# Weight sums at set places in GpSimd's queue, an earlier load of the up block, and a shorter modulation in a two-layer hybrid transformer

## The chip, the cores and the metric

One core of one Trainium2 chip runs the whole kernel. The metric is the device time of one execution in microseconds (us). The engines are TensorE (PE, matrix products; PEld is its weight load), VectorE (DVE), ScalarE (ACT), GpSimd (POOL) and SyncE (SP), whose queue issues all transfers (DMAs) here. Each engine works through its own queue in order and waits on semaphores for the others.

## The reference, cut to what matters

512 latent tokens and 256 context tokens of width 1024 go through two layers. In a layer a conditioning vector gives six modulation vectors; three mixers (window attention, gated linear attention, neighbourhood attention) work on the modulated norm, then comes the feed-forward network (FFN), hidden width 2816. The context is updated in layer 0 only; layer 1 uses it just for keys, values and the context part of the gated linear attention.

```python
def swiglu(h, w_in, w_out):
    gate, up = jnp.split(h @ w_in, 2, axis=-1)
    return (jax.nn.silu(gate) * up) @ w_out
...
    for l in range(DEPTH):
        last = l == DEPTH - 1
        mod = (jax.nn.silu(c) @ w_ada[l] + b_ada[l])[:, None, :]
        mod_c = (jax.nn.silu(c_ctx) @ w_ada[l] + b_ada[l])[None, None, :]
        sh_m, sc_m, gt_m, sh_f, sc_f, gt_f = jnp.split(mod, 6, axis=-1)
        shc_m, scc_m, gtc_m, shc_f, scc_f, gtc_f = jnp.split(mod_c, 6, axis=-1)
        h = rmsnorm(x, norm_mix[l]) * (1.0 + sc_m) + sh_m
        hc = rmsnorm(xc, norm_mix[l]) * (1.0 + scc_m) + shc_m
...
        hf = rmsnorm(x, norm_ffn[l]) * (1.0 + sc_f) + sh_f
        x = x + gt_f * swiglu(hf, w_ffn_in[l], w_ffn_out[l])
        if not last:
            hfc = rmsnorm(xc, norm_ffn[l]) * (1.0 + scc_f) + shc_f
            xc = xc + gtc_f * swiglu(hfc, w_ffn_in[l], w_ffn_out[l])
```

## The kernel before

**Products.** Activations lie with channels on the partitions and tokens in the free direction. Each f32 operand is split into a high and a low part (`fp32r`), and a product is three passes: high weight by high activation, high by low, low by high. A weight block of 128x1024 is loaded by SP into one of three buffers `wr` (line 317), ACT casts its high half `wh` (L346), and DVE subtracts to get the low half `wl` (L350). `run_items` goes through a list of items: it loads as far as buffers allow, splits up to three items ahead, and calls the item's products. Results land in the PSUM tiles `g` and `h` in rotation. Activations are split by ACT (L183) and DVE (L184).

**Seven products.** In the FFN of layer 0 the hidden blocks 3 to 21 (nineteen of them) take seven products of 128x384 where eight would do it directly, in the manner of Strassen and Winograd, over the two halves of the 768 tokens and of the block pair G (gate) and U (up). `seven` writes a block as four items: `i1` (two products from G), `i2` (two, from the sums `ta`), `i3` (two, from half of U and half of `tb`) and `i4` (one, from `tb`). The sums of weights `ta` and `tb` are made by POOL, four operations on 128x512 for each block (L483). `sums()` writes those that have their operands and a free buffer into the program; before, it is called wherever a split is written. The gate block's buffer comes free after the last of the four, the up block's after `i3`'s split. SiLU times up is `evac` (L1830): one operation on POOL for each half of the tokens (x = 0 after `i3`, x = 1 after `i4`).

**Groups.** The blocks are worked in groups of 3, 3, 3, 3, 3, 3 and 4. Behind each comes an output product: eight items `w_fo`, each with 512 and 256 columns, added to the residual by DVE (L1794). The first item `i1` of the next group's first block (`begun`) stands ahead of the output product, the rest behind it.

**Late modulation.** `ada_late` makes the six modulation vectors of layer 1 beside the FFN of layer 0. It takes 96 steps: SP loads a 128x512 block of weights (`wad`, two buffers, L696), DVE multiplies it with the vectors of two streams, latents and context, and adds to `wac` (L706 the first, L708 the others: one operation for each stream). After eight steps sixteen or eight small products with `sel` gather the rows on PE, ACT copies them (`ada`, L721), products with `k_sel` turn them (`o`), and DVE writes `mod` (L757). A step is written into the program when the kernel's own program clock has moved on by the number that the generator yields; what is left at the start of layer 1 is written by `drain` in `close_phase`.

Of the kernel before, what the change touches and what calls it, by code (L numbers as in the profile page):

```python
# [22 lines left out]
KT = D // 128  # L23
# [120 lines left out]
class Net:  # L144
# [155 lines left out]
    def run_items(self):  # L300

        ws = [n for n, it in enumerate(self.items) if it.weights]
        raw, split, early = {}, {}, set()
        st = {"d": 0, "s": 0, "q": 0, "lo": None}

        def load():
            while st["d"] < len(ws):
                it = self.items[ws[st["d"]]]
                if it.w is None:
                    raw[st["d"]] = None  # L310
                    early.add(st["d"])
                    st["d"] += 1
                    continue
                if len({id(t) for q, t in raw.items() if q not in early} | {id(t) for t in self.held}) > 2:
                    break
                t = self.base.tile([128, 1024], F32, tag="wr", name=self.nm("wr"), bufs=3)
                self.nc.sync.dma_start(t[:, :it.nk * 128], it.w)
                raw[st["d"]] = t
                if it.got:
                    it.got(t)  # L320
                st["d"] += 1

        def split_lo():
            f, st["lo"] = st["lo"], None
            if f:
                f()
            self.sums()

        def split_hi(k):

            self.sums()
            while st["s"] < len(ws) and st["s"] <= k:
                q = st["s"]
                it = self.items[ws[q]]
                if it.raw:
                    st["s"] += 1
                    continue
                if st["lo"] or q not in raw or (len(split) > 1 and q != st["q"]):
                    return
                parts = it.parts() if it.parts else [(raw[q], 0, it.nk * 128)]  # L340
                if parts is None:
                    return
                hi = self.base.tile([128, 1024], F32R, tag="wh", name=self.nm("wh"), bufs=3)
                lo = self.base.tile([128, 1024], F32R, tag="wl", name=self.nm("wl"), bufs=3)
                for r, c, n in parts:
                    self.nc.scalar.copy(hi[:, c:c + n], r[:, :n])  # L346

                def lo_part(q=q, it=it, parts=parts, hi=hi, lo=lo):
                    for r, c, n in parts:
                        self.nc.vector.tensor_tensor(out=lo[:, c:c + n], in0=r[:, :n],  # L350
                                                     in1=hi[:, c:c + n].bitcast(F32), op=ALU.subtract)
                    del raw[q]
                    if it.done:
                        it.done()
                    split[q] = (hi, lo)
                st["lo"] = lo_part
                st["s"] += 1

        def ahead(lo=True):
            load()  # L360
            split_hi(st["q"] + 3)
            if lo:
                split_lo()
                load()

        def preload(q, pool=None):
            it = self.items[ws[q]]
            if pool is None:
                t = self.base.tile([128, 1024], F32, tag="wr", name=self.nm("wr"), bufs=3)
            else:  # L370
                t = pool.tile([128, 1024], F32, tag="W0", name=self.nm("W0"), bufs=16)
                early.add(q)
            self.nc.sync.dma_start(t[:, :it.nk * 128], it.w)
            raw[q] = t
            st["d"] = max(st["d"], q + 1)
        self.preload = preload
        self.ahead, self.split_lo = ahead, lambda: (split_lo(), load())
        for it in self.items:
            if not it.weights:
                it.fn()  # L380
                continue
            q = st["q"]
            load()
            if not it.raw:
                split_lo()
                if q not in split:
                    split_hi(q)
                    split_lo()
            load()
            if it.raw:  # L390
                it.fn(raw.pop(q))
            else:
                w = split.pop(q)
                it.fn(*w)
            st["q"] += 1

    def gemm(self, w, nk, subs):

        def sub(wh, wl, mov, n, evac):
            ps = self.gemm_psum()  # L400
            for kt in range(nk):
                xh, xl = mov(kt)
                if any(lo.tensor is xl.tensor for lo, _ in self.late):
                    self.flush()
                s = slice(kt * 128, kt * 128 + 128)
                last = kt == nk - 1
                self.matmul(ps[:, :n], wh[:, s], xh, start=kt == 0, stop=False)
                self.matmul(ps[:, :n], wh[:, s], xl, start=False, stop=False)
                self.matmul(ps[:, :n], wl[:, s], xh, start=False, stop=last)
                if kt == nk // 2 - 1:  # L410
                    self.flush()
                    self.ahead(False)
                if self.clock > self.ticked + self.grain and not last:
                    self.tick()
            self.split_lo()
            evac(ps)
            self.tick()

        def fn(wh, wl):
            for x in subs:  # L420
                sub(wh, wl, *x)
        self.items.append(Item(fn, w, nk))
# [47 lines left out]
    def seven(self, l, wg, wu, h2, evac, end):  # L470
# [9 lines left out]
        def got_u(t):  # L480
# [24 lines left out]
                drop("ta")  # L505
                return True
            self.todo.extend((t12, t34))
            self.sums()

        def drop(k):  # L510
            self.sumt[k] -= 1
# [28 lines left out]
        def i1(wh, wl):  # L540
            ps = product((wh, wl), 0, low, first)
            p = g["p"] = self.T()
            A.copy(p[:, m1], ps)
            self.tick()
            ps = product((wh, wl), 512, high, first)
            s = g["s"] = self.T()
            V.tensor_tensor(out=s[:, m1], in0=p[:, m1], in1=ps, op=ALU.add)
            A.activation(out=s[:, m1], in_=s[:, m1], func=AF.Silu)
            self.tick()

        def i2(wh, wl):
# [9 lines left out]
        def i3(wh, wl):  # L561
            p, s = g["p"], g["s"]
            ps = product((wh, wl), 512, lambda k: self.s3[k // 2], lambda k: (m1, m2)[k % 2])
            V.tensor_tensor(out=s[:, m2], in0=p[:, m1], in1=ps, op=ALU.add)
            P.tensor_tensor(out=p[:, m1], in0=p[:, m1], in1=p[:, m2], op=ALU.add)
            P.tensor_tensor(out=p[:, m2], in0=p[:, m2], in1=s[:, m2], op=ALU.add)
            self.tick()
            ps = product((wh, wl), 0, lambda k: self.s24[k], second)
            V.tensor_tensor(out=p[:, m1], in0=p[:, m1], in1=ps, op=ALU.add)
            evac(0, s, p)  # L570
            self.tick()

        def i4(wh, wl):
# [5 lines left out]
            if end:  # L579
# [1 line left out]
            self.tick()  # L581
        self.items += [
            Item(i1, wg, KT, got=got_g),
            Item(i2, wu, KT, got=got_u, parts=lambda: [(g["ta"], 0, 1024)] if "ta" in g else None,
                 done=lambda: drop("ta")),
            Item(i3, parts=lambda: [(g["U"][:, 512:], 0, 512), (g["tb"], 512, 512)] if "tb" in g else None,
                 done=done_u),
# [98 lines left out]
    def ada_late(self, l):  # L686
# [3 lines left out]
        sb = None  # L690
        todo = [(n, h, kt) for n in range(6) for h in range(2) for kt in range(KT)]

        def load(q):
            n, h, kt = todo[q]
            t = self.ph.tile([128, 512], F32, tag="wad", name=self.nm("wad"), bufs=2)
# [3 lines left out]
        for q, (n, h, kt) in enumerate(todo):  # L699
            nxt = load(q + 1) if q + 1 < len(todo) else None  # L700
            if kt == 0:
                acc = self.ph.tile([128, 2, 512], F32, tag="wac", name=self.nm("wac"), bufs=1)
            for s in range(2):
                c = self.cpad[:, kt, s:s + 1]
                if kt == 0:
                    nc.vector.tensor_scalar(out=acc[:, s], in0=w, scalar1=c, scalar2=None, op0=ALU.mult)  # L706
# [1 line left out]
                    nc.vector.scalar_tensor_tensor(out=acc[:, s], in0=w, scalar=c, in1=acc[:, s], op0=ALU.mult,  # L708
                                                   op1=ALU.add)
            w = nxt  # L710
            yield 4.5
            if kt < KT - 1:
                continue
            ps = self.gemm_psum()
            for s in range(2):
                for g in range(4):
                    self.matmul(ps[32 * g:32 * g + 32, :128], self.sel[:, s], acc[:, s, 128 * g:128 * g + 128],
                                start=s == 0, stop=s == 1, tile_position=(0, 32 * g))
            if h == 0:
                sb = self.base.tile([128, 256], F32, tag="ada", name=self.nm("ada"), bufs=1)  # L720
            nc.scalar.copy(sb[:, 128 * h:128 * h + 128], ps[:, :128])  # L721
# [1078 lines left out]
    def ffn_items(self, l, ntok):  # L1800
# [24 lines left out]
        def seven(t):  # L1825
            h2 = ntok // 2

            def evac(x, s, u):
                w = (slice(0, h2), slice(h2, ntok))[x]
                nc.gpsimd.tensor_tensor(out=s[:, w], in0=s[:, w], in1=u[:, w], op=ALU.mult)  # L1830
                if x == 0:
                    st["u"].append((self.T(F32R, "T2"), self.T(F32R, "T2")))
                hi, lo = st["u"][-1]
# [5 lines left out]
        for gi, (t0, tn) in enumerate(groups):  # L1839
# [19 lines left out]
            w = lambda j: self.a["w_fo"][l, j][:, t0 * 128:(t0 + tn) * 128]  # L1859
            if gi < len(groups) - 1:  # L1860
                for j in range(8):
                    self.gemm(w(j), tn, [(self.mov(lambda: st["u"], c[0], c[1]), c[1] - c[0],
                                          lambda ps, j=j, c=c: self.resid(l, GT_F, j, c, ps, False))
                                         for c in subs_of])
# [144 lines left out]
```

## Time and profile before

| | |
|---|---|
| time, median of 3 runs | 2558.26 us (2554.17 to 2559.53) |
| the profiled execution, its time | 2560.89 us |
| its span in the trace | 2559.1 us |
| mean granted clock of PE | 0.983 |
| busy: PE | 2429.3 us (95%) |
| busy: DVE | 1667.7 us (65%) |
| busy: ACT | 1104.6 us (43%) |
| busy: POOL | 591.3 us (23%) |

The span is the time between the first and the last instruction in the trace; all times of rows are counted from its start. An engine's busy time is the sum of its instructions; what is missing to the span is waiting. The FFN stretch with seven products runs from about 1004 to 1468 us, layer 1 begins at about 1547 us.

### The profile page before, as it was taken

To read this page: it belongs to the slowest core of one execution; us is meant where nothing else is said; L and a number is where in the kernel's file an instruction comes from. 1 tells how busy PE (TensorE), PEld (TensorE's weight loads), DVE (VectorE), ACT (ScalarE), POOL (GpSimd) and SP (SyncE) were. 2 spreads that over 40 slices of the span, in tenths; PEclk is the share of its full clock that TensorE was granted. 3 is DMA by queue.
4 is the path that set the end of the run, shared out by engine and by line. 5 is a ranking of instruction groups with operands and counts; after the bars stand their busy time and mean duration, and the time that the engine had idled before them with its cause. 6 is when DMAs were issued, how large, how long until landed. Compare 5 with 4: busy or idle time off the path is not lost. (4 is left out here: it accounts for less than half of the span.)

```text
span 2559.1 us, 40070 instructions
## 1 busy us (share of the span) xinstructions
PE 2429.3 (95%) x15128; PEld 2076.6 (81%) x15128; DVE 1667.7 (65%) x3240; ACT 1104.6 (43%) x1866; POOL 591.3 (23%) x610
## 2 busy tenths in 40 slices
PE   6999999999999999899999887999999999999998
PEld 3777888988878888888888865777888879888887
DVE  4675366647667678887878786857657668633336
ACT  3543345546554353233223344535545565522223
POOL 0231123213203025354433512312313220000000
PEclk8999999999999999999999998999999999999999
DMA  6443542222157331332333252224322266433233
GB/s 219 144 132 117 179 120 72 85 90 66 58 181 240 108 120 59 105 98 95 118 103 112 83 169 88 75 91 119 104 95 81 89 228 193 142 98 98 91 95 120
DMA packets 127954, 299.51 MB, mean 117 GB/s; under 512 B 22800, under 2 KB 38928, under 8 KB 127760
## 3 DMA queue, kind: packets, MB, share of 16 engines
q1 hardware_dynamic: 127760, 296.95, 36.4%
q8 instruction: 119, 1.95, 0.3%
q14 instruction: 75, 0.61, 0.1%
HBM read 257.56 MB, written 29.57 MB: 112 GB/s over the span
## 5 line engine op out<-in xcount | busy, mean ns | idle before, releaser
L221 PE MATMUL g<-T,wh 128*128 128x512 f32 (+2 forms) x4588 | 1227.9, 354 | 11.8 <-ACT T L183 7.3
L221 PEld LDWEIGHTS g<-T,wh 128*128 128x128 f32 x4588 | 795.3, 191 | 123.0 <-issue 17.5
L221 PE MATMUL g<-T,wl 128*128 128x512 f32 (+2 forms) x2294 | 802.8, 350 | 21.9 <-DVE wl L350 21.9
L221 PE MATMUL h<-T,wh 128*128 128x512 f32 (+2 forms) x2556 | 660.8, 345 | 11.6 <-ACT T L178 7.7
L346 ACT CAST wh<-wr 128x1024 fp32r<-128x1024 f32 (+3 forms) x387 | 341.3, 883 | 577.4 <-PE g L221 205.3
L350 DVE TENSOR_TENSOR wl<-wr,wh 128x1024 fp32r<-128x1024 f32 (+3 forms) x387 | 413.6, 1069 | 213.9 <-ACT wh L346 199.0
L221 PEld LDWEIGHTS h<-T,wh 128*128 128x128 f32 x2556 | 449.4, 190 | 66.8 <-ACT T L178 9.4
L221 PEld LDWEIGHTS g<-T,wl 128*128 128x128 f32 x2294 | 437.6, 191 | 79.5 <-DVE wl L350 26.5
L221 PE MATMUL h<-T,wl 128*128 128x512 f32 (+2 forms) x1278 | 439.7, 344 | 9.2 <-DVE wl L350 8.9
L221 PEld LDWEIGHTS h<-T,wl 128*128 128x128 f32 x1278 | 242.2, 190 | 36.3 <-DVE wl L350 13.5
L1514 POOL TENSOR_SCALAR P<-P,sm 128x512 f32<-128x512 f32 (+1 forms) x160 | 113.9, 713 | 366.1 <-DVE sm L1513 336.2
L1509 ACT ACTIVATE P<-P,sm 128x513 f32<-128x513 f32 (+3 forms) x160 | 116.2, 727 | 127.1 <-DVE sm L1551 115.9
L708 DVE SCALAR_TENSOR_TENSOR wac<-wad,cpad,wac 128x512 f32<-128x512 f32 x168 | 149.4, 913 | 10.5 <-DMA wad<-in_w_ada_dram 10.1
L1564 DVE TENSOR_TENSOR ptl<-s,pth 128x512 fp32r<-128x512 f32 (+1 forms) x144 | 107.9, 749 | 39.2 <-ACT pth L1563 38.0
L183 ACT CAST T<-T 128x512 fp32r<-128x512 f32 (+2 forms) x93 | 49.3, 538 | 153.4 <-POOL T L1830 140.0
L1563 ACT CAST pth<-s 128x512 fp32r<-128x512 f32 (+1 forms) x144 | 90.8, 630 | 48.7 <-PE s L225 43.6
L1160 POOL TENSOR_TENSOR E<-E,T 128x512 f32<-128x512 f32 (+1 forms) x42 | 62.8, 1507 | 203.8 <-ACT E L1156 144.1
L225 PE MATMUL s<-k_ident,P 128*128 128x128 f32 x640 | 94.2, 274 | 4.2 <-POOL P L1514 2.2
L1794 DVE SCALAR_TENSOR_TENSOR T<-h,mod,T 128x512 f32<-128x512 f32 (+1 forms) x98 | 59.0, 608 | 57.1 <-PE h L221 56.5
L225 PEld LDWEIGHTS s<-k_ident,P 128*128 128x128 f32 x640 | 74.4, 140 | 20.0 <-issue 7.3
L892 POOL TENSOR_TENSOR T<-T,T 128x256 f32<-128x256 f32 (+1 forms) x24 | 29.9, 1271 | 245.5 <-issue 92.6
L184 DVE TENSOR_TENSOR T<-T,T 128x512 fp32r<-128x512 f32 (+2 forms) x93 | 58.1, 632 | 35.8 <-ACT T L183 35.3
(246 smaller groups left out, 2771.6 us busy)
## 6 DMA issues: line engine op xcount, KB each, us to landing
wr<-in_w_fi_dram SPq DMA_DIRECT2D x98, 512.0 KB, 3.5
wr<-in_w_in_dram SPq DMA_DIRECT2D x65, 512.0 KB, 3.8
wr<-in_w_merge_dram SPq DMA_DIRECT2D x48, 512.0 KB, 3.9
wad<-in_w_ada_dram SPq DMA_DIRECT2D x96, 256.0 KB, 2.7
wr<-in_w_ada_dram SPq DMA_DIRECT2D x32, 512.0 KB, 4.4
wr<-in_w_out_dram SPq DMA_DIRECT2D x32, 512.0 KB, 3.7
wr<-in_w_br_dram SPq DMA_DIRECT2D x48, 256.0 KB, 2.8
T<-zd SPq DMA_DIRECT2D x24, 384.0 KB, 4.1
```

Source lines behind the costliest of these rows:

```text
L184: self.late.append((lo, lambda: self.nc.vector.tensor_tensor(out=lo, in0=src, in1=hi.bitcast(F32), op=ALU.subtract)))
L221: return self.nc.tensor.matmul(out, lhsT, rhs, **kw)
L225: return self.nc.tensor.transpose(out, src, self.ident)
L346: self.nc.scalar.copy(hi[:, c:c + n], r[:, :n])
L350: self.nc.vector.tensor_tensor(out=lo[:, c:c + n], in0=r[:, :n], in1=hi[:, c:c + n].bitcast(F32), op=ALU.subtract)
L708: nc.vector.scalar_tensor_tensor(out=acc[:, s], in0=w, scalar=c, in1=acc[:, s], op0=ALU.mult, op1=ALU.add)
L1160: P.tensor_tensor(out=ee[:, 1, c0:c1], in0=ee[:, 1, c0:c1], in1=self.gk[p][:, t0:t0 + c1 - c0], op=ALU.mult)
L1509: nc.scalar.activation(out=P_[:, o0:e1], in_=P_[:, o0:e1], func=AF.Exp, bias=nm_, accum_out=rz)
L1514: nc.gpsimd.tensor_scalar(out=P_[:, o0:o1], in0=P_[:, o0:o1], scalar1=rz, scalar2=1.0, op0=ALU.mult, op1=ALU.mult)
L1563: nc.scalar.copy(hi, src)
L1564: return lambda: VE.tensor_tensor(out=lo, in0=src, in1=hi.bitcast(F32), op=ALU.subtract)
L1794: self.nc.vector.scalar_tensor_tensor(out=x[:, c0:c1], in0=ps[:, :c1 - c0], scalar=self.mod[l][:, sec * 8 + j, s:s + 1], in1=x[:, c0:c1], ...
```

## The change

It has four parts, none of which changes what is computed for the output.

1. `sums()` is no longer called where weights are split, but at three set places: behind a product's evacuation in `gemm` (so in an output product), behind `i1`'s SiLU, and behind the second evacuation of `i3`. So POOL's queue has the four sums of a block together.
2. The up block gets an item of its own without products (`raw`), between `i1` and `i2`. With `begun` this item is put into the output product ahead of its fifth `w_fo` item.
3. In the last layer `ada_late` computes only the latents' stream for the modulation vectors n = 2 to 5 (of context tokens layer 1 needs only the first two). 64 of the 96 steps have one operation on `wac` instead of two: 192 operations become 128, and 32 fewer `sel` products follow. A step yields 4.0 instead of 4.5.
4. The second half of `evac` (x = 1) is done by DVE instead of POOL.

```diff
         def split_lo():
...
-            self.sums()
 
         def split_hi(k):
 
-            self.sums()
...
             self.split_lo()
             evac(ps)
+            self.sums()
             self.tick()
...
             self.todo.extend((t12, t34))
-            self.sums()
...
             A.activation(out=s[:, m1], in_=s[:, m1], func=AF.Silu)
+            self.sums()
             self.tick()
...
             evac(0, s, p)
+            self.sums()
             self.tick()
...
-            Item(i2, wu, KT, got=got_u, parts=lambda: [(g["ta"], 0, 1024)] if "ta" in g else None,
+            Item(lambda t: None, wu, KT, raw=True, got=got_u),
+            Item(i2, parts=lambda: [(g["ta"], 0, 1024)] if "ta" in g else None,
                  done=lambda: drop("ta")),
...
+        streams = lambda n: range(1 if l == DEPTH - 1 and n > 1 else 2)
+
...
-            for s in range(2):
+            for s in streams(n):
                 c = self.cpad[:, kt, s:s + 1]
...
-            yield 4.5
+            yield 4.0
...
-                nc.gpsimd.tensor_tensor(out=s[:, w], in0=s[:, w], in1=u[:, w], op=ALU.mult)
+                (nc.gpsimd, nc.vector)[x].tensor_tensor(out=s[:, w], in0=s[:, w], in1=u[:, w], op=ALU.mult)
...
                 for j in range(8):
+                    if j == 4 and begun:
+                        self.items.append(begun.pop(0))
```

Line numbers of the changed kernel are up to four higher in this part (L712 for L708, L761 for L757, L1834 for L1830).

**How often `wac` stands in DVE's order.** Counted to the row that splits `ta` of a block (`wl<-ta`): ahead of the sixth of the nineteen blocks 53 operations before and 59 now, ahead of the seventh 64 and 72, ahead of the last 160 and 118, and in all 192 and 128.

**First place: DVE at the end of layer 0's work and the start of layer 1.** Before, the last operations on `wac` (from the blocks `wad`) stand between the splits `wl` of layer 1's first weights, directly ahead of `mod` and of `gm`, the mask of the gated linear attention:

```order
L350 TENSOR_TENSOR wl_15080<-wr_14958,wh_15079 128x1024
L350 TENSOR_TENSOR wl_15117<-wr_15031,wh_15116 128x1024
L708 SCALAR_TENSOR_TENSOR wac_15090<-wad_15135,cpad,wac_15090 128x512 x2
L708 SCALAR_TENSOR_TENSOR wac_15090<-wad_15139,cpad,wac_15090 128x512 x2
L350 TENSOR_TENSOR wl_15256<-wr_15052,wh_15255 128x1024
L708 SCALAR_TENSOR_TENSOR wac_15090<-wad_15143,cpad,wac_15090 128x512 x2
...
L708 SCALAR_TENSOR_TENSOR wac_15090<-wad_15155,cpad,wac_15090 128x512 x2
L757 TENSOR_TENSOR mod_80<-o_15171,bada_728 128x16
L938 CAST gm_15183<-E_15184 128x384
```

Now the last three stand amid the norm (`nsm` its row statistics, T<-T,mod its result):

```order
L712 SCALAR_TENSOR_TENSOR wac_14529<-wad_14949,cpad,wac_14529 128x512
L892 SCALAR_TENSOR_TENSOR T_14793<-T_14794,mod_80,T_14792 128x512
L899 TENSOR_TENSOR T_14807<-T_14808,T_14806 128x512
L195 TENSOR_SCALAR nsm_14853<-nsm_14853 128x2
L712 SCALAR_TENSOR_TENSOR wac_14529<-wad_15017,cpad,wac_14529 128x512
L198 TENSOR_TENSOR nsm_14853<-nsm_14853 128x2
L199 SCALAR_TENSOR_TENSOR nsm_14853<-nsm_14853 128x2
L200 SCALAR_TENSOR_TENSOR nsm_14853<-nsm_14853 128x2
```

and what stands between there and the same `mod` and `gm` is the rest of the norm and splits:

```order
L348 TENSOR_TENSOR wl_15015<-wr_14905,wh_15014 128x1024
L348 TENSOR_TENSOR wl_15050<-wr_14977,wh_15049 128x1024
L761 TENSOR_TENSOR mod_80<-o_15075,bada_728 128x16
L942 CAST gm_15087<-E_15088 128x384
L348 TENSOR_TENSOR wl_15160<-wr_14998,wh_15159 128x1024
L348 TENSOR_TENSOR wl_15193<-wr_15033,wh_15192 128x1024
```

The last operation on `wac` is 29 rows ahead of `mod`. On PE, the first product from the gate weights (`s<-T,gw`) comes 35 rows behind the last `o<-k_sel,ada` instead of 22.

**Second place: SP in the third group's output product.** Before, from the third of the eight `w_fo` items on; the three `w_fi` blocks are the up block of the next group's first block and the next pair:

```order
L317 DMA wr_11363<-in_w_fo_dram 128x384
L317 DMA wr_11387<-in_w_fo_dram 128x384
L696 DMA wad_11655<-in_w_ada_dram 128x512
L317 DMA wr_11425<-in_w_fo_dram 128x384
L317 DMA wr_11457<-in_w_fo_dram 128x384
L317 DMA wr_11485<-in_w_fo_dram 128x384
L317 DMA wr_11517<-in_w_fo_dram 128x384
L317 DMA wr_11545<-in_w_fi_dram 128x1024
L317 DMA wr_11553<-in_w_fi_dram 128x1024
L317 DMA wr_11585<-in_w_fi_dram 128x1024
```

Now, from the third `w_fo` item on again:

```order
L317 DMA wr_11371<-in_w_fo_dram 128x384
L317 DMA wr_11395<-in_w_fo_dram 128x384
L317 DMA wr_11433<-in_w_fi_dram 128x1024
L317 DMA wr_11446<-in_w_fo_dram 128x384
L317 DMA wr_11473<-in_w_fo_dram 128x384
L317 DMA wr_11511<-in_w_fo_dram 128x384
L700 DMA wad_11580<-in_w_ada_dram 128x512
L700 DMA wad_11629<-in_w_ada_dram 128x512
L317 DMA wr_11549<-in_w_fo_dram 128x384
L700 DMA wad_11673<-in_w_ada_dram 128x512
L700 DMA wad_11719<-in_w_ada_dram 128x512
L317 DMA wr_11577<-in_w_fi_dram 128x1024
```

The up block (the first `w_fi`) has moved from behind the eighth `w_fo` item to between the fourth and the fifth; the sixth item waits for the gate block's buffer.

**Third place: POOL in the fourth group.** L565 and L566 are the sums of activations in `i3`, L1830 the two products of `evac`. Before:

```order
L483 TENSOR_TENSOR tb_11696<-wr_11585 128x512
L483 TENSOR_TENSOR tb_11696<-wr_11553,ta_11613 128x512
L565 TENSOR_TENSOR T_11389<-T_11389 128x384
L566 TENSOR_TENSOR T_11389<-T_11389,T_11408 128x384
L1830 TENSOR_TENSOR T_11408<-T_11408,T_11389 128x384
L483 TENSOR_TENSOR ta_11780<-wr_11735,wr_11665 128x512
L483 TENSOR_TENSOR ta_11780<-wr_11735,ta_11780 128x512
L1830 TENSOR_TENSOR T_11408<-T_11408,T_11389 128x384
L483 TENSOR_TENSOR tb_11848<-wr_11735 128x512
L483 TENSOR_TENSOR tb_11848<-wr_11665,ta_11780 128x512
```

Now:

```order
L483 TENSOR_TENSOR tb_11760<-wr_11608 128x512
L483 TENSOR_TENSOR tb_11760<-wr_11577,ta_11640 128x512
L565 TENSOR_TENSOR T_11397<-T_11397 128x384
L566 TENSOR_TENSOR T_11397<-T_11397,T_11416 128x384
L1834 TENSOR_TENSOR T_11416<-T_11416,T_11397 128x384
L483 TENSOR_TENSOR ta_11828<-wr_11763,wr_11670 128x512
L483 TENSOR_TENSOR ta_11828<-wr_11763,ta_11828 128x512
L483 TENSOR_TENSOR tb_11909<-wr_11763 128x512
L483 TENSOR_TENSOR tb_11909<-wr_11670,ta_11828 128x512
L565 TENSOR_TENSOR T_11810<-T_11810 128x384
L566 TENSOR_TENSOR T_11810<-T_11810,T_11825 128x384
```

The second product has left POOL, and the four sums of the next block follow the first product without a break.

## Rows read from the trace of the kernel before

**Rows 1.** The page's busy times: engine, us, share, instructions.
```profile
PE 2429.3 (95%) x15128; PEld 2076.6 (81%) x15128; DVE 1667.7 (65%) x3240; ACT 1104.6 (43%) x1866; POOL 591.3 (23%) x610
```

**Rows 2.** Table of stages: length, busy times, granted clock, DMA share, GB/s.
```profile
1004.00:1057.00 53.00, 43.47 (x228) 40.27 (x228) 48.57 (x58) 17.39 (x31) 34.55 (x23) 0.90 0.31 97
1135.00:1166.00 31.00, 26.86 (x136) 22.97 (x135) 19.55 (x31) 5.85 (x12) 8.23 (x7) 0.89 0.31 98
1166.00:1480.00 314.00, 292.59 (x1707) 270.58 (x1706) 250.36 (x349) 100.38 (x180) 141.97 (x102) 0.99 0.34 105
1547.40:1569.00 21.60, 9.44 (x46) 6.95 (x45) 10.10 (x16) 1.70 (x3) 2.39 (x5) 0.68 0.45 155
```

**Rows 3.** PE's waits: 1000 to 1560, 1004 to 1166, 1166 to 1480.
```profile
PE g L221 <- DVE wl L350: 16.3, 9, 3.5
PE g L221 <- DVE wac L708: 12.2, 1, 12.2
PE h L221 <- DVE wl L350: 8.9, 8, 3.1
...
PE g L221 <- DVE wl L350: 9.0, 4, 3.5
...
PE h L221 <- DVE wl L350: 7.7, 6, 3.1
PE g L221 <- DVE wl L350: 7.4, 5, 2.2
PE g L221 <- ACT T L183: 3.5, 1, 3.5
```

**Rows 4.** Timeline at layer 1's start: start, us, instruction, idle before.
```profile
1552.89 2.74 DVE L708 SCALAR_TENSOR_TENSOR wac<-wad,cpad,wac 128x512 f32<-128x512 f32 x4 [0.83 <-DMA wad<-in_w_ada_dram]
...
1557.80 2.74 DVE L708 SCALAR_TENSOR_TENSOR wac<-wad,cpad,wac 128x512 f32<-128x512 f32 x4 [2.17 <-DMA wad<-in_w_ada_dram]
...
1559.93 1.32 PE L221 MATMUL g<-wac,sel 128*32 128x128 f32 x16 [12.16 <-DVE wac L708]
...
1564.37 1.05 PE L221 MATMUL g<-T,wh 128*128 128x512 f32 x2
...
1566.70 0.62 PE L221 MATMUL g<-T,wh 128*128 128x512 f32 x2
```

**Rows 5.** L708's durations (ns min/median/max); all `wac` work, 1166 to 1480.
```profile
L708 DVE SCALAR_TENSOR_TENSOR wac<-wad,cpad,wac x168: 736/748/1839, 748.9 to 1559.8; 128x512 f32<-128x512 f32 x168
...
1166.00:1480.00 314.00, 91.13 (x101) 0.99 0.34 105
```

**Rows 6.** DVE's groups, 1000 to 1480: busy us, mean ns.
```profile
L569 DVE TENSOR_TENSOR T<-T,h 128x384 f32<-128x384 f32 x16 | 8.8, 549 | 10.8 <-POOL T L565 9.2 <-PE h L221 1.6
...
L461 DVE TENSOR_TENSOR T<-T,T 128x384 fp32r<-128x384 f32 x4 | 5.9, 1465 | 0.0
```

**Rows 7.** Third output product, timelines; then loads (KB, us to landing).
```profile
1142.72 1.29 POOL L1830 TENSOR_TENSOR T<-T,T 128x384 f32<-128x384 f32 x1 [2.30 <-ACT T L577]
1163.04 1.32 POOL L483 TENSOR_TENSOR ta<-wr,wr 128x512 f32<-128x512 f32 x1 [19.04 <-DMA wr<-in_w_fi_dram]
...
1145.52 0.55 DVE L350 TENSOR_TENSOR wl<-wr,wh 128x384 fp32r<-128x384 f32 x1
...
1152.10 0.62 PE L221 MATMUL h<-T,wh 128*128 128x512 f32 x2
...
1155.25 0.62 PE L221 MATMUL h<-T,wh 128*128 128x512 f32 x2
...
1155.33 0.51 ACT L346 CAST wh<-wr 128x384 fp32r<-128x384 f32 x1 [2.59 <-PE h L221]
...
wr<-in_w_fi_dram SPq DMA_DIRECT2D x98, 512.0 KB, 3.5
...
wr<-in_w_fo_dram SPq DMA_DIRECT2D x48, 192.0 KB, 2.4
```

More of the change, by code (lines that the diff above doesn't have):

```diff
@@ L570, in i3 @@
             evac(0, s, p)
+            self.sums()
             self.tick()
@@ L714, in ada_late @@
             ps = self.gemm_psum()
-            for s in range(2):
+            for s in streams(n):
                 for g in range(4):
                     self.matmul(ps[32 * g:32 * g + 32, :128], self.sel[:, s], acc[:, s, 128 * g:128 * g + 128],
-                                start=s == 0, stop=s == 1, tile_position=(0, 32 * g))
+                                start=s == 0, stop=s == streams(n)[-1], tile_position=(0, 32 * g))
             if h == 0:
```

## The prediction

> **What bounds the kernel now.** I read the page's busy table first. TensorE (PE) is busy 2429.3 us, 95% of the span; the next engine, VectorE (DVE), has 65% [rows 1]. So a change pays only where PE stands still or runs at the lower clock. The table of stages [rows 2] shows where that is: in the first stage of three blocks by seven products DVE is busy 48.57 of 53 us and PE 43.47; over the later groups, 1166 to 1480 us, PE has 292.59 of 314 and DVE still 250.36. At the start of layer 1 PE is busy only 9.44 of 21.6 us, at a granted clock of 0.68. The list of PE's waits [rows 3] says what ends its gaps: between 1000 and 1560 us the low halves of the weights that DVE makes (L350), 16.3 + 8.9 us, and one single wait of 12.2 us for `wac` (L708), the late modulation of layer 1; smaller ones for the split activations (L183).
>
> **The change, part by part. a) The drain at layer 1.** In the timeline [rows 4] PE stands 12.16 us before sixteen small `sel` products at 1559.93, because DVE still does eight operations on `wac`, two for each 256 KB block of `wad`, and waits 0.83 and 2.17 us for those blocks to land. After that PE is at half speed for a while: two 512-wide products take 1.05 us at 1564.37 where two take 0.62 us at 1566.70. The 5.5 us from the end of the `sel` products (1559.93 + 1.32) to 1566.70 would be 3.2 us at that ratio; 2.3 us are lost. In the order after the change the last operation on `wac` stands amid the layer's norm, 29 rows ahead of `mod`, and each of the last `wad` blocks wants one operation instead of two. The wait loses its cause: −12.2 − 2.3 = **−14.5** (bounds −10, if DVE or the blocks are still some us late, and −16). What is late next is the gate chain of the GLA mixer behind `gm`; in PE's queue the first product from its weights, `s<-T,gw`, comes 35 rows behind the modulation's last `o` instead of 22, and 13 products are some 4 us (0.62 for two that overlap). They have to be done anyway; for a later start of that chain I charge **+1** (0 to +3).
>
> **b) Half of the later operations on `wac`.** From 1166 to 1480 us DVE does 101 of them in 91.13 us, 0.90 each [rows 5]. By the counts in the order (given with the change) there are 46 instead of 96 over the twelve blocks from the seventh on, so about 53 of the 101 go: −48 us of DVE's 250.36. Against this stand thirteen products that it takes from POOL (c), 12 us. DVE falls from 80% to 68% there. PE's waits in the same stretch are 7.7 + 7.4 us for L350 and 3.5 for L183 [rows 3], 18.6 in all. Those are bursts: several operations of 0.75 to 1.84 us [rows 5] stand ahead of a split in DVE's queue, and half of them go. I take somewhat over half of the waits, **−11** (0 to −21, with what the clock gives back). Before 1166 the number hardly moves (59 against 53 by the sixth block, 72 against 64 by the seventh, the extra ones beside an output product).
>
> **c) The second product of a block on DVE.** Nineteen operations on 128x384 leave POOL, 1.29 us apiece where nothing disturbs it [rows 7]. The price on DVE lies between 0.549 us (L569, the same size) and 1.465 us (L461, the same size with both operands in SBUF, much of it beside a busy POOL) [rows 6]. A SiLU on ACT stands before it, an operation on as many columns as the cast of 0.51 [rows 7]; DVE's queue waits for it unless the one or two rows between cover it. I take 0.9 with the wait. In the six blocks before 1166, where DVE has little room and PE waits 9.0 us for L350 [rows 3], this is 6 × 0.9 = 5.4 us more; less POOL work beside DVE's operations gives part of it back: **+2** (0 to +6). After 1166 it is netted in (b). At the end of a group the chain of SiLU, product and L183 becomes 1.29 − 0.55 = 0.74 us shorter; where PE waits for it, in one group in two or so, that is **−2** (0 to −4).
>
> **d) The up block and its sums amid the output product.** In the third group [rows 7] the buffer that the up block now takes comes free when the third `w_fo` item is split, at 1145.52 + 0.55. Its load lands 3.5 us later, at 1149.6; four sums of 1.32 end at 1154.9; then the gate block's buffer is free, and the sixth `w_fo` item is loaded (2.4), cast (0.51) and split (0.55): ready at 1158.4. On PE the third and the fourth item start at 1152.10 and 1155.25, 3.15 apart, so the sixth is wanted at 1161.55. The slack of 3.1 us hides it, as the fourth and fifth are split already. Where POOL or DVE is some us late, as may be in the first output product, it is gone. For six output products I take **+2.5** together (0 to +9, half an item's time each). That the sums are done earlier gains nothing: PE doesn't wait for `ta` now. SP issues in order, and behind the sixth item's load stand `wad` blocks and the last two items, which wait with it.
>
> **The rest.** 32 `sel` products of 128 columns fewer, a small fraction of 1.32 us for each sixteen with their loads [rows 4]: at most 2.6 us in all, spread where PE often waits anyway. I count nothing.
>
> Sum: −14.5 + 1 − 11 + 2 − 2 + 2.5 = −22. The profiled execution took 2560.89 us, 1.8 more than its span and 2.6 more than the median of the three runs; taken off the median, 2558.26 − 22 = 2536.3, the forecast is **2536**.
>
> **A rule against the change.** L708 takes 0.736 us at the least and up to 1.839 [rows 5], on the same operands: operations of DVE with two inputs in SBUF get longer while POOL works. In the new order four sums stand right behind the first product on POOL, so the second one, on DVE some 3 us later (twelve 384-wide products, an addition, a SiLU), meets them. The Trainium skill ("SBUF — State Buffer", section "Who interferes with whom") says that a DVE instruction with two SBUF inputs contends with a GpSimd instruction that reads SBUF, and that the one that comes second is blocked for the other's whole instruction. The spread above agrees in kind. By the rule each of the nineteen costs what L461 shows or more, and POOL's sums wait as well.
>
> **The rivals.** *R1, DVE is not relieved:* every product collides, 19 × (1.465 + 0.51) = 38 us come onto DVE and eat most of the 48. Terms b and c become −2 and +5, and the result is 2558.3 − 14.5 + 1 − 2 + 5 − 2 + 2.5 = 2548. For it: the spread of L708. Against: POOL loses nineteen operations, so meets DVE less. *R2, more:* the waits for L350 and L183 from 1166 on vanish with the dips of the clock behind them, and (d) and (c) cost nothing: −14.5 − 21 − 2 + 1 gives 2522. *R3, slower:* the output products stall. From the up block's load on, one buffer of three turns over until the sums are done. If POOL starts them late, or that load waits on SP behind `wad` blocks, each us beyond the slack is PE's, and the clock falls with it: a granted 0.89 over the 31 us from 1135 to 1166 [rows 2], behind a wait, is 3.4 us of work. It decides from 24.5 / 6 = 4.1 us a group on, which means sums 4 to 7 us later than reckoned; at 7 us a group it is 2558.3 − 24.5 + 42 = 2576. Against it: POOL has nothing to do between 1144.0 and 1163.0 [rows 7]. *R4, the drain only moves:* operations on `wac` that stand ahead of the norm's small rows on DVE delay those, and some 10 of the 14.5 us turn up as waits for the norm or for `gm`: 2546; with R1 as well, no change.
>
> **How the numbers follow.** Forecast (2527 to 2544) 0.60; R1 or R4 alone (2544 to 2552) 0.19; R2 (under 2527) 0.11; R1 with R4 (no change) 0.05; R3 0.05. A measurement of this kernel tells about 0.2%, 5 us, from no change. So faster 0.88, same 0.06 and slower 0.06 (a little of the edge between the cases to each). Leaving out a tenth on either side gives 2518 to 2551.
>
> **What would show it.** a: PE's wait for `wac` is gone, and the 512-wide products of layer 1 follow each other without a gap at full clock. b: DVE is some 36 us less busy from the seventh block to the end of the stage, and PE's waits for L350 there halve. c: the new product on DVE has a mean near 0.6 (the forecast) or 1.5 (R1). d: in no output product does PE wait for a split behind POOL's `tb`; if it does, R3. The prediction is wrong if PE waits for L350 as long with half of the `wac` work gone, since then something else than the bursts makes DVE late, or if the 12 us come back within layer 1's first stage.

## The result and the profile after

The changed kernel takes 2524.47 us (median of 4 runs, 2522.52 to 2525.91); beside the kernel before in the same runs (2558.9) the ratio is 0.9869 [0.9852, 0.9886], so 33.5 us less (29 to 38). The forecast was 22 less, the range 7 to 40 less. The direction is right and the size within the range; about a quarter of the gain came from a place where I had expected none.

The page's busy times and the table of stages (length, busy us of PE, PEld, DVE, ACT, POOL, granted clock, DMA share, GB/s), for the stretch that answers to 1166 to 1480 [rows 2] and for the start of layer 1:

```profile
PE 2423.0 (96%) x15064; PEld 2073.9 (82%) x15064; DVE 1622.9 (64%) x3195; ACT 1102.9 (44%) x1866; POOL 564.2 (22%) x591
```

```profile
1166.00:1462.00 296.00, 289.32 (x1647) 270.21 (x1646) 215.14 (x314) 100.98 (x180) 123.72 (x87) 0.99 0.37 115
1525.00:1537.00 12.00, 12.00 (x62) 10.17 (x62) 4.70 (x7) 3.96 (x6) 0.00 (x0) 1.00 0.65 213
```

In that stretch DVE is busy 215.14 us instead of 250.36, 35 less (36 forecast), and PE stands 6.7 us instead of 21.4; the stretch is 18 us shorter, 14.7 of them less standing and 3.3 less work. At the start of layer 1 PE is busy all the time, at full clock (1.00). PE's waits, from 1164 to 1460 (from 1166 to 1462 the list is the same), and below them the timeline of PE at the place of the old drain:

```profile
PE o L221 <- ACT ada L725: 3.0, 1, 3.0
PE h L221 <- ACT T L183: 2.9, 2, 2.0
PE h L221 <- DVE wl L348: 0.6, 1, 0.6
```

```profile
1526.74 0.29 PE L221 MATMUL o<-k_sel,ada 128*128 128x8 f32 x2
1526.88 0.72 PE L221 MATMUL g<-T,wh 128*128 128x512 f32 x2
```

Of 15.1 us of waiting for the low halves in that stretch [rows 3] 0.6 is left. The `o` products are followed by the first 512-wide ones without a gap; before, PE stood 12.16 us ahead of the last `sel` products at this place [rows 4]. One wait has grown: 3.0 us for ACT's copy of `ada`, against 0.4 before.

**Where the time went.** To see where the two executions come apart, I matched PE's products of both traces in their order and took the difference of the starts (after less before, us) at a few places of the kernel before. The same for runs that are told of below:

```
place in the kernel before           after     e1     e4     e6     e2     e9    e12    e10     e3     e8
981   ahead of the product stages     -1.5    0.3    1.0   -3.5    0.0   -3.7   -3.1   -3.5   -4.2    0.5
1001  first output product             3.9    5.3    1.4   -3.5    4.7    2.0    2.3    1.3   -3.8    6.4
1057  blocks 1 to 3                   -0.1   -1.0    1.5   -6.1    2.6   -1.5   -1.0   -5.4   -2.6    0.4
1171  blocks 4 to 6, third product    -2.1   -2.7    1.1   -7.5    0.0   -0.9   -4.8  -12.3   -4.4   -0.2
1321  blocks 10 to 12, fifth product -11.6   -5.2   -7.5   -8.3   -7.5   -9.0  -12.1  -24.7  -14.5  -11.6
1500  last group                     -19.9  -10.8  -11.2  -11.9  -14.1  -12.4  -18.9  -40.2  -20.3  -16.6
1546  ahead of the drain             -20.8  -10.8   -9.5  -12.1  -14.5  -13.4  -19.9  -41.0  -20.9  -11.3
1562  behind the drain               -34.9  -10.9  -23.6  -12.0  -28.7  -27.5  -34.1  -55.1  -35.1  -25.1
1636  layer 1                        -33.8  -10.8  -22.7  -11.9  -27.5  -26.4  -34.6  -55.6  -35.6  -23.5
```

These are single executions, and already at 981, ahead of the stages that were changed, they differ by some us; those of e4 and e8 took 5 and 7 us longer than the medians of their runs. The drain is the step of 14.1 from 1546 to 1562. The rest, some 19 us, grows beside the seven products, most of it from 1171 on, where `wac` is halved.

### The profile page after: what moved, and what is told of

Its sections match the earlier page's. It is cut to its first block, busy times and chain, and to the rows that moved or that the text cites. A ratio compares the mean times of both kernels' runs of the same rounds, so it can differ in the third digit from the quotient of the medians.

```text
span 2523.7 us, 39840 instructions
## 1 busy us (share of the span) xinstructions
PE 2423.0 (96%) x15064; PEld 2073.9 (82%) x15064; DVE 1622.9 (64%) x3195; ACT 1102.9 (44%) x1866; POOL 564.2 (22%) x591
## 5 line engine op out<-in xcount | busy, mean ns | idle before, releaser
L221 PEld LDWEIGHTS g<-T,wh 128*128 128x128 f32 x4604 | 797.9, 191 | 110.1 <-issue 11.5
L221 PE MATMUL g<-T,wl 128*128 128x512 f32 (+2 forms) x2302 | 804.4, 350 | 14.2 <-DVE wl L348 14.1
L348 DVE TENSOR_TENSOR wl<-wr,wh 128x1024 fp32r<-128x1024 f32 (+3 forms) x387 | 421.6, 1089 | 248.5 <-ACT wh L344 236.8
L712 DVE SCALAR_TENSOR_TENSOR wac<-wad,cpad,wac 128x512 f32<-128x512 f32 x112 | 98.1, 886 | 18.0 <-DMA wad<-in_w_ada_dram 17.6
L183 ACT CAST T<-T 128x512 fp32r<-128x512 f32 (+2 forms) x93 | 49.2, 537 | 117.2 <-POOL T L1834 85.1
L184 DVE TENSOR_TENSOR T<-T,T 128x512 fp32r<-128x512 f32 (+2 forms) x93 | 57.8, 629 | 33.4 <-ACT T L183 33.1
```

The costliest lines, as they stand in the source:

```text
L184: self.late.append((lo, lambda: self.nc.vector.tensor_tensor(out=lo, in0=src, in1=hi.bitcast(F32), op=ALU.subtract)))
L221: return self.nc.tensor.matmul(out, lhsT, rhs, **kw)
```

## The experiments

All ratios are to the kernel before, run beside each; its medians were 2558.3 to 2560.1 us.

| run | what differs | ratio [95% interval] | median us |
|---|---|---|---|
| after | the change | 0.9869 [0.9852, 0.9886] | 2524.47 |
| e1 | after, two streams again | 0.9954 [0.9942, 0.9967] | 2548.13 |
| e2 | after, second product on POOL again | 0.9891 [0.9876, 0.9905] | 2533.37 |
| e3 | after, up block behind the output product | 0.9872 [0.9858, 0.9887] | 2526.74 |
| e4 | before, one stream alone | 0.9898 [0.9883, 0.9913] | 2533.35 |
| e5 | after, sums at the old places | 0.9863 [0.9846, 0.9881] | 2523.06 |
| e6 | before, second product on DVE alone | 0.9962 [0.9950, 0.9975] | 2549.05 |
| e7 | after, both products on DVE | 0.9814 [0.9799, 0.9828] | 2512.27 |
| e8 | after, rows of the modulation turned later | 0.9900 [0.9883, 0.9918] | 2531.38 |
| e9 | after, a spare product on POOL | 0.9909 [0.9895, 0.9923] | 2536.23 |
| e10 | e7, and L565, L566 on DVE | 0.9795 [0.9781, 0.9809] | 2507.57 |
| e11 | e7, sums at the old places | 0.9804 [0.9791, 0.9818] | 2510.07 |
| e12 | after, fills on POOL | 0.9870 [0.9849, 0.9891] | 2527.23 |

### The late modulation: e1 and e4

```diff
-        streams = lambda n: range(1 if l == DEPTH - 1 and n > 1 else 2)
+        streams = lambda n: range(2)
...
-            yield 4.0
+            yield 4.5
```

> The changed kernel with both streams in all 96 steps of the late modulation again, and the old yield of 4.5; the other three parts stay. Theory A (half of the wac work gives the drain and most of the gain beside the seven products): the wait of PE for wac at layer 1's start is back with 10 to 13 us, DVE is some 45 us busier, PE waits for L350 again in the stages from the seventh block on; the time is 2524.5 + 13.5 + 10 to 16 = 2548 to 2554. Rival B (the sums in one piece and the second product off POOL give the gain beside the seven products): only the drain comes back, 2524.5 + 13.5 = 2538.

> The kernel before with the shorter modulation alone (one stream for n = 2 to 5 in layer 1, yield 4.0). Theory A: the drain goes (13.5) and most of the gain beside the seven products comes, 10 to 16: 2558.5 - 23.5 to 29.5 = 2529 to 2535. Rival B: the drain alone, 2545.

e4 is part 3 of the change, put into the kernel before. Both went as theory A said: the part alone gives 26 us (22 to 30), and without it 22 (by the ratios) to 24 us (by the medians) of the change's gain are gone. In e1's timeline the drain is back:

```profile
1549.08 1.32 PE L221 MATMUL g<-wac,sel 128*32 128x128 f32 x16 [12.07 <-DVE wac L712]
```

The table above splits it: 14 us at the drain, and 9 to 12 beside the products (e4 from +1.0 at 981 to −11.2 at 1500; after less e1 at 1500, 9.1). Of the 15.1 us of waiting for the low halves [rows 3], e4 has 1.4 left (1160 to 1470 of its trace):

```profile
PE h L221 <- DVE wl L350: 1.0, 2, 0.8
...
PE g L221 <- DVE wl L350: 0.4, 1, 0.4
```

In the same stretch of e4 PE waits 5.1 us for L183; e1, with the other three parts and all of `wac`, has 8.6 us of waiting for the low halves. A smaller share of the 9 to 12 is the `sel` products. The page counts 64 instructions fewer on PE (15128 against 15064), as each of the 32 products is two in the trace; at 0.64 us for sixteen, which the changed kernel's timeline has at 1002.53, I estimate 2.6 us for them.

### The second product: e2, e6

```diff
-                (nc.gpsimd, nc.vector)[x].tensor_tensor(out=s[:, w], in0=s[:, w], in1=u[:, w], op=ALU.mult)
+                nc.gpsimd.tensor_tensor(out=s[:, w], in0=s[:, w], in1=u[:, w], op=ALU.mult)
```

> The changed kernel with the second product of a block on POOL again; the other three parts stay. Theory A (the product costs DVE 0.55 us and shortens the chain SiLU, product, L183 at a group's end by 0.7 to 1.4 us, and POOL gets in DVE's way less): 3 to 8 us slower, 2527 to 2533, with the stalls of 3 to 4 us ahead of the output products back. Rival C (nineteen operations more on DVE, with the wait for the SiLU, were a price that the other parts paid for): 3 us faster or more, 2521 or less.

> The kernel before with the second product of a block on DVE and nothing else changed. Theory A (on POOL it lengthens DVE's operations with two operands in SBUF and holds the sums and L183 up; on DVE it costs 0.55 us and meets nothing): 6 to 9 us faster than the kernel before, 2550 to 2553. Rival B (it pays only once the late modulation leaves DVE room): within 3 us of the kernel before, 2556 to 2562.

Both came out within 1 us of theory A's numbers. e6 is 9.7 us faster than the kernel before (6 to 13); e2 loses 6 (by the ratios) to 9 us (by the medians). So the product on DVE pays by itself. That it pays on top of the rest as well is likely but less sure, since the intervals of e2 and of the changed kernel overlap at their edges. The page's line of e6:

```profile
PE 2423.0 (95%) x15128; PEld 2073.2 (81%) x15128; DVE 1667.1 (65%) x3259; ACT 1103.1 (43%) x1866; POOL 564.4 (22%) x591
```

DVE has nineteen operations more than before and is busy no longer: 1667.1 against 1667.7 us [rows 1]. The product by itself, in the changed kernel (ns min/median/max):

```profile
L1834 POOL TENSOR_TENSOR T<-T,T x19: 1263/1987/1999, 1032.2 to 1445.8; 128x384 f32<-128x384 f32 x19
L1834 DVE TENSOR_TENSOR T<-T,T x19: 543/551/559, 1038.1 to 1449.5; 128x384 f32<-128x384 f32 x19
```

Nineteen times 0.55 is 10.5 us, so other operations of DVE became 11 us shorter. Which ones shows the list of DVE's groups (busy us, mean ns), 980 to 1480, first of e6, then of the kernel before:

```profile
L708 DVE SCALAR_TENSOR_TENSOR wac<-wad,cpad,wac 128x512 f32<-128x512 f32 x134 | 122.4, 933 | 4.3 <-DMA wad<-in_w_ada_dram 4.2
...
L350 DVE TENSOR_TENSOR wl<-tb,wh 128x512 fp32r<-128x512 f32 x38 | 29.8, 784 | 0.0
```

```profile
L708 DVE SCALAR_TENSOR_TENSOR wac<-wad,cpad,wac 128x512 f32<-128x512 f32 x129 | 121.3, 963 | 4.6 <-DMA wad<-in_w_ada_dram 4.4 <-DVE wl L350 0.2
...
L350 DVE TENSOR_TENSOR wl<-tb,wh 128x512 fp32r<-128x512 f32 x38 | 34.4, 906 | 0.0
```

The splits of `tb` went from 906 to 784 ns, `wac` from 963 to 933. L569, which reads one operand from PSUM, has the same mean in both (549 [rows 6] and 548).

How the second product lengthened the splits of `tb` can be read from the kernel before, by the times of both. Six of these splits started 0.51 to 0.52 us behind the product on POOL and took 1.48 to 1.50 us; the product, which had itself started beside an earlier split, took 1.44 to 1.47. Six others started 0.18 to 0.19 us ahead of it; they took 0.68 to 0.69 us, as they do with POOL idle, and POOL's product then took 1.37 us, where the three products that met no operation of DVE took 0.99 to 1.00. So in these meetings the one that starts second gets longer. A meeting of the first kind, POOL and DVE:

```profile
1109.51 1.47 POOL L1830 TENSOR_TENSOR T<-T,T 128x384 f32<-128x384 f32 x1
...
1110.03 1.50 DVE L350 TENSOR_TENSOR wl<-tb,wh 128x512 fp32r<-128x512 f32 x1
```

Six times 0.8 us are 4.8 us, about what the splits of `tb` lost in e6 (34.4 to 29.8). How much of the 9.7 us PE got through DVE and how much through the shorter chain from the SiLU to L183 was not taken apart: from 980 to 1480 PE's waits for L350 fall from 26.3 to 23.1 us, and those for L183 from 9.3 to 5.8.

### What of POOL costs: e9 and e12

Either POOL's work lengthens DVE's operations, or the wait for the product holds the later sums up in POOL's queue. Both kernels leave the real product on DVE and put something at the old place in POOL's queue that nobody waits for, e9 a product, e12 fills:

```diff
+                if x:
+                    nc.gpsimd.tensor_tensor(out=self.ph.tile([128, 352], F32, tag="spare", name=self.nm("spare"), bufs=1), in0=s[:, h2:h2 + 352], in1=u[:, h2:h2 + 352], op=ALU.mult)
```

```diff
+                if x:
+                    for _ in range(3):
+                        nc.gpsimd.memset(u[:, w], 0.0)
```

> The changed kernel with a spare product on POOL at the place in its queue where the second product of a block was: of 352 columns, into a tile that nobody reads; DVE still does the real one. So POOL is as busy as in the run with the second product on POOL, and reads SBUF at the same time, but no split waits for it. Theory A (POOL's work itself is the cost: it lengthens DVE's operations with operands in SBUF and puts the later sums back): most of the 6 to 9 us of that run come back, 2530 to 2534, and DVE is some 10 us busier than in the changed kernel (1622.9 us). Theory B (the shorter chain SiLU, product, L183 is the gain): no change, 2523 to 2527.

> The changed kernel with three fills of 128x384 on POOL at the place in its queue where the second product was (they overwrite an operand that nobody reads any more, behind DVE's product). POOL is held up at the same place as in the run with the spare product, for which the trace shows 50.7 us of waiting for DVE's product in nineteen cases, and is busy there for about as long, but reads nothing from SBUF. Theory A (what costs is POOL's reading beside DVE's operations): 2523 to 2528 as the changed kernel, and L184 on DVE has a mean near 645 ns as there, not 886 as with the spare product. Theory B (what costs is POOL's queue: the sums behind the waiting instruction come later): 2531 to 2537, with L184 at 645 ns as well, and PE waiting for L348 and L344 behind the sums.

e9 is 10 to 12 us slower than the changed kernel, 2 us beyond theory A's numbers; e12 is the same (0.9870 against 0.9869). POOL is held up equally in both; their rows of POOL's waits, e9 and then e12:

```profile
POOL spare L1836 <- DVE T L1834: 50.7, 19, 3.4
```

```profile
POOL T L1837 <- DVE T L1834: 50.3, 19, 3.4
```

It isn't the queue, then. The groups of DVE differ where the spare product meets the split of the activations, L184 (e9, then e12; the changed kernel has 645 ns):

```profile
L184 DVE TENSOR_TENSOR T<-T,T 128x384 fp32r<-128x384 f32 x38 | 33.7, 886 | 31.0 <-ACT T L183 31.0
```

```profile
L184 DVE TENSOR_TENSOR T<-T,T 128x384 fp32r<-128x384 f32 x38 | 24.5, 644 | 31.0 <-ACT T L183 31.0
```

One such meeting in e9's timeline, POOL and DVE:

```profile
1110.59 1.41 POOL L1836 TENSOR_TENSOR spare<-T,T 128x352 f32<-128x352 f32 x1 [1.70 <-DVE T L1834]
...
1111.09 1.32 DVE L184 TENSOR_TENSOR T<-T,T 128x384 fp32r<-128x384 f32 x1
```

L184 takes 1.32 us beside POOL's reading; its median in the kernel before was 0.559. In all eighteen meetings of the two in e9, L184 starts second and ends 0.41 to 0.42 us after the spare product. Fills that take longer (three of 419 ns against one of 965, medians) do nothing: beside them L184 never takes more than 0.56 us. PE's list in e9 names L184 for 1.9 us of waiting; for the rest of the 10 to 12 us no single wait stands out. The meetings at L184 are e9's own. In the kernel before, the second product met the splits of `tb` and `wac`, and L184 had a mean of 653 ns. So e9 and e12 show that POOL's reading costs and its queue doesn't; they don't measure what the reading cost there. The Trainium skill ("SBUF — State Buffer", section "Who interferes with whom") says that a DVE instruction with two SBUF inputs contends with a GpSimd instruction that reads SBUF and not with one that only writes it; e9 and e12 agree with both halves.

### The early up block and the sums: e3, e5

```diff
-                    if j == 4 and begun:
-                        self.items.append(begun.pop(0))
```

> The changed kernel with the up block's load behind the output product again (as an item of its own, sums at the set places). Theory A (the early load makes DVE's queue and the sixth item late in the output products: +5 us in the first, +1.7 in the second, +3.8 in the fourth by the comparison of the traces, of which some comes back in the stage behind): these go, the stages that follow start as late as before; 4 to 8 us faster, 2517 to 2521. Rival D (the early sums are what takes the gaps out of the stages of seven products): 4 us slower or more, 2529 or above.

> The changed kernel with the sums of weights called at the old places again (wherever a split is written, and when the up block is loaded); the other three parts stay, the early up block too. Theory A (the set places are worth little; the three parts without the shorter modulation gave 10.8 us in the trace, of which the second product on DVE 6 to 9): 0 to 4 us slower than the changed kernel, 2524 to 2528. Rival B (the four sums in one piece are what makes the difference): 6 us slower or more, 2530 or above.

e5 puts the three old calls of `sums()` in place of the three new ones; a fourth new call, in `run_items` ahead of a split that comes late, stays. Neither moves the time beyond its interval, so both theories on e3 fall: the early load neither costs nor gains. PE's timeline shows why, first of the changed kernel, then of e3:

```profile
995.37 0.80 PE L221 MATMUL g<-T,wl 128*128 128x512 f32 x1 [4.16 <-DVE wl L348]
```

```profile
1009.16 1.01 PE L221 MATMUL h<-T,wh 128*128 128x384 f32 x2 [4.01 <-ACT wh L344]
```

With the up block early, the first output product stalls 4.16 us; without, the stall of 4.01 comes behind it, where `i2` waits for `ta`. By the matched starts the changed kernel loses 5.4 us from 981 to 1001 and e3 0.4, but by 1057 the two have lost 1.4 and 1.6. DVE's timeline of the changed kernel has a split of 128x384 that takes 1.65 us there, beside POOL's sums, instead of 0.55 [rows 7]:

```profile
993.67 1.65 DVE L348 TENSOR_TENSOR wl<-wr,wh 128x384 fp32r<-128x384 f32 x1
```

### Going on: e7, e10, e11, and e8

```diff
-                (nc.gpsimd, nc.vector)[x].tensor_tensor(out=s[:, w], in0=s[:, w], in1=u[:, w], op=ALU.mult)
+                nc.vector.tensor_tensor(out=s[:, w], in0=s[:, w], in1=u[:, w], op=ALU.mult)
...
-            P.tensor_tensor(out=p[:, m1], in0=p[:, m1], in1=p[:, m2], op=ALU.add)
-            P.tensor_tensor(out=p[:, m2], in0=p[:, m2], in1=s[:, m2], op=ALU.add)
+            V.tensor_tensor(out=p[:, m1], in0=p[:, m1], in1=p[:, m2], op=ALU.add)
+            V.tensor_tensor(out=p[:, m2], in0=p[:, m2], in1=s[:, m2], op=ALU.add)
```

e7 has the first of these edits, e10 both, e11 the first and the old calls of `sums()`; e8 stands alone:

```diff
-            yield 1.5
+            yield 1.5 if h == 0 else 4.0
```

> The changed kernel with the first product of a block on DVE too. Theory A (POOL at work lengthens DVE's operations, and what leaves POOL relieves both): the product costs 0.55 us on DVE instead of some 2 us on POOL, 2 to 6 us faster, 2518 to 2522. Rival B (DVE is the narrower engine beside the seven products, and POOL's first product hindered it little): no change or up to 5 us slower, 2524 to 2530.

> The kernel with both products of a block on DVE (2512) and the two sums of activations in i3 (L565, L566) on DVE as well, so that POOL has only the sums of weights left in the FFN. Theory A (POOL at work hinders DVE more than the operation costs DVE): 38 operations of 0.55 us come to DVE, but their 2 times 1.1 us on POOL go and the chain to the first product gets shorter by 1.1 us: 3 to 8 us faster, 2504 to 2509. Rival B (DVE is the narrower engine by now): 0 to 8 us slower, 2512 to 2520.

> The kernel with both products of a block on DVE (2512) with the sums of weights called at the old places. If the set places are worth nothing, as the run with the sums at the old places alone says, it is the same within 3 us, 2509 to 2515; if they serve once POOL is less busy, 4 us slower or more.

> The changed kernel with the turning of the modulation's rows (the products with k_sel) written later behind ACT's copy: the program clock moves on by 4.0 instead of 1.5 between them. It tests whether the new wait of PE for ACT's copy (3.0 us in the changed kernel, none worth naming before) is a cost of its own. Theory A: PE's wait for L725 goes, 3 us faster, 2521.5. Rival B: the wait stands where PE would have waited for the split activations anyway; no change, 2524 to 2526.

e7 gives 14 us more by the ratios (12 by the medians), twice what I expected at most; e10 is at 0.9795 [0.9781, 0.9809], 52 us under the kernel before. That is the lowest of all, but its interval overlaps those of e7 and e11. Pages of e7 and e10:

```profile
PE 2418.5 (96%) x15064; PEld 2071.1 (82%) x15064; DVE 1630.6 (65%) x3214; ACT 1103.4 (44%) x1866; POOL 534.4 (21%) x572
```

```profile
PE 2407.3 (96%) x15064; PEld 2064.3 (82%) x15064; DVE 1648.7 (66%) x3252; ACT 1104.8 (44%) x1866; POOL 484.6 (19%) x534
```

In e7 DVE is busy 7.7 us longer than in the changed kernel for nineteen operations that are 10.5 at 0.55, in e10 25.8 us longer for 57 operations that are 31.4. So DVE gets back only a part of their price here, and something else must pay too; the chain behind `i3` is the likeliest. ACT's L183 waited 85.1 us in all for POOL's first product in the changed kernel and 18.5 for DVE's second; in e7 it waits 75.5 for both, and PE's waits for L183 (980 to 1500) fall from 4.7 to 0.3 us. The shares of the two in e7 and e10 weren't taken apart. e11 again shows the places of the sums to be worth nothing.

e8 came out as neither theory said: PE's wait for L725 is gone from its list, yet it is 7 (by the medians) to 8 us (by the ratios) slower, with an interval that just touches the changed kernel's. By the matched starts it is 2 us ahead of the changed kernel at 1452 of the kernel before, 4 us behind at 1480 and 9 to 10 behind at 1546. So a good half of the loss comes at the end of the last group, ahead of its output product. There PE waits 3.7 us for L183, and the granted clock is 0.86 (1446 to 1458 of e8's trace). DVE's timeline of e8 has three operations on `wac` from 1444 to 1451, where the changed kernel's has none, so the later turning seems to have moved later steps into this place. The rest comes where layer 1's norm is made; I think that the modulation comes too late for it. Neither cause was tested by a run.

## Why the prediction came out as it did

**a, the drain: right.** −14.5 + 1 forecast, 14.1 measured at the place, and e1 brings it back. The late start of the gate chain cost 1 us at most (−34.9 to −33.8 by 1636; e12 and e10 lose nothing there). R4 did not come.

**b, half of `wac`: right in mechanism and size.** −11 forecast, −9 to −12 by e1 and e4. PE's waits for the low halves fell further than the half that I had named as a sign, from 15.1 to 1.4 us in e4, where PE still waits for L183; in the changed kernel both waits are small. Some 2.6 us of the −9 to −12 belong to the `sel` products by the estimate above, a term that I had put at nothing.

**c, the second product: the term that failed.** I had put +2 and −2, nothing in sum; alone it gives −9.7 (e6), on top of the rest −6 to −9 (e2). Two things were wrong in it. The price: 0.55 on DVE in all nineteen cases (543 to 559 ns), at the lower bound. I had added a meeting and the wait for the SiLU, and argued from the order of the rows that the product meets the four sums; in the trace POOL is idle during all nineteen. My 1.29 us for the product on POOL "where nothing disturbs it" was a wrong reading as well: DVE's L708 ran beside it from 1142.40 to 1143.15, and undisturbed it takes 0.99 to 1.00. And the relief: I wrote that less POOL work "gives part of it back", and it gave all of it back and more. What I set against the change, that DVE's operations get longer beside POOL's reading, holds (e9, e12), and so does the blocking of the one that comes second, in the meetings told above. But it spoke for this edit, which takes nineteen readers off POOL. R1 priced the meetings of the one new operation; that POOL would meet DVE's old ones less often it named without a price.

**d, the up block and the sums: right that it costs little.** +2.5 forecast, 0 measured (e3, e5). The stall that I bounded does come, in the first output product, but it takes the place of one behind it. R3 did not come: behind the first output product PE waits at most 2.3 us at a time for L348, and 0.6 us in all from 1164 to 1460.

So the sum was off by 11.5 us: by e2 and e6 6 to 10 of them are c's, and 2.5 are d's. The range held; the likeliest range did not (2527 to 2544), and the result lies in R2's. As R2 said, the waits for L350 and L183 after 1166 nearly vanished (18.6 to 3.5 us). R2 gave no cause for the second half of them; the runs show one, that DVE's operations also got shorter (e6).

## What to carry to other kernels

When an operation moves from GpSimd to VectorE, count both sides: its price there, and what VectorE's other two-operand instructions lose while GpSimd reads. The spread between the least and the longest duration of one and the same instruction (0.74 to 1.84 us here) is where that loss is read. A stall that an earlier transfer seems to cause may only be one that was taken from the next stage: compare the same product's start some stages later, not the list of waits.

## What was unexpected of the hardware

Nineteen elementwise products on GpSimd that nobody waited for cost 10 to 12 us of 2524, with VectorE's L184 going from 645 to 886 ns in the mean, while fills at the same place, of no less time, cost nothing. In the kernel before, the 115 operations of L708 with GpSimd idle took 0.74 to 0.76 us, and the 53 beside a working GpSimd up to 1.84, with a median of 1.36. Operations with one operand in PSUM (L569) kept a mean of 548 to 552 ns in the runs with GpSimd's products on either engine.
